# Seven products instead of eight for seven pairs of K tiles in the right half of a down projection

## The chip, the cores and the metric

The kernel runs on one core of a Trainium2 chip. The metric is the device time of one execution in microseconds; lower is better. TensorE is called PE here, VectorE DVE, ScalarE ACT, GpSimd POOL and SyncE SP, as in the profile.

## The reference

Two layers of a decoder trunk on 256 positions of width 2048, all in float32. The change touches the MLP at the end of each layer:

```python
hm = _rmsnorm(x, mlp_norm_g[l]) @ w_up[l]                # 256 x 2048 @ 2048 x 8192
x = x + jnp.square(jax.nn.relu(hm)) @ w_down[l]          # 256 x 8192 @ 8192 x 2048
```

Before it stand an attention and a short convolution with projections of their own (`w_in`, `w_out`); they are the same in both kernels.

## The kernel before

Every float32 matrix is split into a high part and a remainder, `hi` and `lo`, and a product is made of three matmuls (`TERMS`: hi by hi, hi by lo, lo by hi). ACT writes `hi` (a copy into a type that PE takes in one pass), DVE writes `lo = raw - hi`. The raw weights come by DMAs that SP issues.

The 256 rows are two tiles of 128, and K = 8192 is 64 tiles of 128, or 32 pairs of two. The MLP of a layer has these stages:

- The up loop, `for i in range(NP)` with NP = 32. A round makes one pair of activation tiles: two column blocks of `w_up` (`up_part`, L809), `evict` (L819, L820) and `square` (L826 to L841), which writes the squared tile to DRAM (`hid`, L831, on POOL's queue) and, for all but the last two pairs, four sums S1 to S4 of its quarters beside the quarters A11 to A22. It splits the eight into `f`.
- In the same loop, two rounds late (LAG = 2), the left half of the down projection (columns 0 to 1023 of `w_down`). A pair is a 2 by 2 block product: two row tiles, two K tiles, two column blocks of 512. Instead of eight products of 128x128 by 128x512 it takes seven (Strassen's scheme in Winograd's form), each of three matmuls (`product`, L849), into seven banks of PSUM. The weights' sums and differences are made by `quarters`: `plain` gives b11, b21 and b22 (tiles b1 and b2), `sums` gives t1 and t3 (t13), `more` gives t2 and t4 (t24). `t` is the tile of the raw sums. The raw pair is the tile `draw`, from a pool with two buffers (`dpool`).
- The last two pairs of the left half go by eight products (L935), straight onto the banks where four of the seven products add up. Then `onto` (L916) and, on POOL, four adds (L927) bring the seven banks into x.
- The right half (columns 1024 to 2047), by eight products for all 32 pairs (L969), in blocks of four K tiles (KG = 4). A block's activations are read back from `hid` (`block`: the tile `back`, split into `g`). A raw tile of 1 MB holds four K tiles by 512 columns, from `upool`, which has three buffers.

`Weights` is a queue of jobs; a job loads a raw tile where one begins and splits it. `take()` hands out the next job's tiles and makes jobs up to three further on (AHEAD). The tiles `whi` and `wlo` (a half of an ordinary pair) and `uhi` and `ulo` (`w_up`) share three buffers each, the tiles of `quarters` have one (b1 two), `f` two, `h` one.

PE's order is the order of the program. On the other engines and on SP a scheduler places each instruction by its estimate of when the operands and buffers are there; on the chip every engine then takes its instructions in that fixed order, and waits at the head of its queue.

Of the kernel before, what the change touches and what calls it, by code (L numbers as in the profile page):

```python
# [9 lines left out]
F32 = mybir.dt.float32  # L10
F32R = mybir.dt.float32r
# [4 lines left out]
P = 128  # L16
# [16 lines left out]
AHEAD = 3  # L33
NP = DFF // (2 * P)
LAG = 2
NB2 = DFF // (KG * P)

# [64 lines left out]
def trunk(ctx: ExitStack, tc: tile.TileContext, x, w_in, w_out, conv_w, q_norm_g, k_norm_g,  # L102
# [162 lines left out]
    class Weights:  # L265
# [3 lines left out]
        def __init__(self, pool):  # L269
            self.pool = pool  # L270
            self.jobs, self.made, self.used = [], [], 0
            self.early = []
# [394 lines left out]
    def mlp(l, mnorm, last):  # L667
# [3 lines left out]
        with ExitStack() as scope:  # L671
# [11 lines left out]
            def column(i, c, kh):  # L683
                def make():
                    if c == 0:
                        raws[kh] = upool.tile([P, 8, 2 * P], F32, tag="uraw", name="uraw")
                        nc.sync.dma_start(
                            raws[kh], w_up[l][kh * 8 * P:(kh + 1) * 8 * P,
                                              i * 2 * P:(i + 1) * 2 * P].rearrange(
                                                  "(k p) c -> p k c", p=P))  # L690
                    hi = wpool.tile([P, 8, P], F32R, tag="hi", name="uhi")
                    lo = wpool.tile([P, 8, P], F32R, tag="lo", name="ulo")
                    src = raws[kh][:, :, c * P:(c + 1) * P]
                    nc.scalar.activation(hi, src, AF.Copy)  # L694
                    nc.vector.tensor_sub(lo, src, hi.bitcast(F32))  # L695
                    return hi, lo
                weights.jobs.append(make)
# [8 lines left out]
            def quarters(i):  # L706


                keep = late if i == 0 else lambda ins: None
# [7 lines left out]

                def plain():
                    raw = forms["raw"] = load_rows(i, 0).rearrange("p k (n c) -> p k n c", n=2)
# [19 lines left out]
                if i == 0:  # L739
                    made = {}  # L740
                    begin = lambda: made.update(p=plain(), s=sums())
                    forms["begin"] = begin
                    return lambda: made["p"], lambda: made["s"], more
                return plain, sums, more

            def rows(i, k, box):
                def make():
                    if k == 0:
                        box.append(load_rows(i, 0))
                    return weights.halves(box[0][:, k].rearrange("p (n c) -> p n c", n=2))  # L750
                weights.jobs.append(make)
# [14 lines left out]
            for i in range(NP - LAG, NP):  # L766
                box = []
                rows(i, 0, box)
                rows(i, 1, box)

            order = [(b - n, n) for b in range(NB2 + 1) for n in range(2) if 0 <= b - n < NB2]

            def four(b, n, k, box):
                def make():
                    if k == 0:
                        raw = upool.tile([P, KG, CH], F32, tag="uraw", name="raw")
                        nc.sync.dma_start(
                            raw, w_down[l][b * KG * P:(b + 1) * KG * P,  # L780
                                           (2 + n) * CH:(3 + n) * CH].rearrange(
                                               "(k p) c -> p k c", p=P))
                        box.append(raw)
                    return weights.halves(box[0][:, k:k + 2])
                weights.jobs.append(make)

            for b, n in order:
                box = []
                four(b, n, 0, box)
                four(b, n, 2, box)  # L790


            hid = [dram.tile([P, KG * S], F32, name=f"hid{l}{b}") for b in range(NB2)]

# [27 lines left out]
            def square(i, h):  # L822
# [8 lines left out]
                nc.gpsimd.dma_start(hid[i // 2][:, i % 2 * 2 * S:(i % 2 + 1) * 2 * S], u)  # L831
                n = 4
                if i < NP - LAG:
                    n = 8
                    nc.vector.tensor_add(h[:, S1], h[:, A21], h[:, A22])
# [10 lines left out]
            def product(n, j, a, b, stop=False):  # L846

                for m, (pa, pw) in enumerate(TERMS):
                    nc.tensor.matmul(prods[n], fs[j][:, pa, a], b[pw], start=(j == 0 and m == 0),  # L849
                                     stop=(stop and m == 2))  # L850
# [49 lines left out]
            first.close()  # L900
            gpool = scope.enter_context(tc.tile_pool(name="gpool", bufs=3))
# [11 lines left out]
            blocks = {0: block(0)}  # L913

            def onto(dst, p, base):
                nc.vector.scalar_tensor_tensor(dst, p, mnorm.scale, base,  # L916
                                               op0=ALU.mult, op1=ALU.add)

            x11, x21, x12, x22 = (xs[n][:, t] for n in range(2) for t in range(NT))
            e1, e2, e3, e4 = wide("e1"), wide("e2"), wide("e3"), wide("e4")  # L920
            nc.scalar.activation(e1, prods[1], AF.Copy, scale=mnorm.scale)
            onto(e2, prods[6], e1)
            onto(e4, prods[5], e2)
            onto(x22, prods[5], x22)
            onto(e3, prods[7], e2)
            for dst, v in ((x11, e1), (x12, e4), (x21, e3), (x22, e3)):
                nc.gpsimd.tensor_tensor(dst, dst, v, op=ALU.add)  # L927

            prods[8] = ps.tile([P, CH], F32, tag="av", name=f"pr{l}8", bufs=1)
            for j in range(NP - LAG, NP):  # L930
                for k in range(2):
                    b = weights.take()
                    for n, t, p in ((0, 0, 2), (0, 1, 4), (1, 0, 3), (1, 1, 8)):
                        for m, (pa, pw) in enumerate(TERMS):
                            nc.tensor.matmul(  # L935
                                prods[p], fs[j][:, pa, 2 * k + t], b[pw][:, n],
                                start=(p == 8 and j == NP - LAG and k == 0 and m == 0),
                                stop=(j == NP - 1 and k == 1 and m == 2))
                    work.tick()
            for dst, p in ((x11, 2), (x21, 4), (x12, 3), (x22, 8)):  # L940
                onto(dst, prods[p], dst)

            def store(n):
                for t in range(NT):
                    nc.sync.dma_start(
                        out[0, t * P:(t + 1) * P, n * CH:(n + 1) * CH], xs[n][:, t])

            if last:
                store(0)
                store(1)  # L950
            else:
                work.start(norm.chunk(0, 2), 12)
                work.start(norm.chunk(1, 2), 24)


            accs = {}
            for b, n in order:
                if n == 0:
                    if b + 1 < NB2:
                        blocks[b + 1] = block(b + 1)  # L960
                if b == 0:
                    accs[n] = mm.tile([P, NT, CH], F32, tag="mm2", name=f"dn{l}{n}")
                f, acc = blocks[b], accs[n]
                for kp in range(KG // 2):
                    hi, lo = weights.take()
                    for k in (2 * kp, 2 * kp + 1):
                        for t in range(NT):
                            for m, (pa, pw) in enumerate(TERMS):
                                nc.tensor.matmul(  # L969
                                    acc[:, t], f[:, pa, k, t * P:(t + 1) * P],  # L970
                                    (hi, lo)[pw][:, k % 2],
                                    start=(b == 0 and k == 0 and m == 0),
                                    stop=(b == NB2 - 1 and k == KG - 1 and m == 2))
                        work.tick()
# [52 lines left out]
```

## Time and profile before

| | |
|---|---|
| median of 3 runs (lowest to highest) | 2178.97 us (2178.82 to 2180.45) |
| profiled execution | 2181.14 us, its span 2179.4 us |
| granted PE clock over the span | 0.999 |
| PE busy | 2156.6 us, 99% |
| DVE, ACT, POOL busy | 74%, 58%, 6% |
| moved by DMA | 446.62 MB, 205 GB/s |

The span is from the profiled execution's first instruction to its last; the rows of the profile count from its start. A busy PE is not PE at its peak, since matmuls overlap and their ends are modelled; so the pace of matmuls is read from their number in a stretch without a wait. The first layer's MLP lies at 400 to 1088 us (the right half of the down projection from 919), the second's from 1480 to the end.

### The profile page before, as it was taken

Reading aid. Unit: us, or ns where it says so; the run is one execution under the profiler, and the core shown is the slowest. Engines: PE = TensorE matmul, PEld = TensorE weight load, DVE = VectorE, ACT = ScalarE, POOL = GpSimd, SP = SyncE. Lnnn points to the kernel's source line nnn. Section 1 sums busy time; section 2 is a strip of 40 time slices with the busy share of each in tenths; the row PEclk is TensorE's granted clock in tenths of the full one; section 3 lists DMA queues with packets and bytes.
Section 4 is the critical chain, followed back from the end, with each engine's and each line's share of the span. In section 5 each row is a group of like instructions: output and inputs, shape, how many; then the busy total and the mean of one; then the engine's idle time right before and its main releaser. Section 6 shows DMA issues by size and latency. Waiting matters only on the chain.

```text
span 2179.4 us, 29050 instructions
## 1 busy us (share of the span) xinstructions
PE 2156.6 (99%) x11066; PEld 1828.6 (84%) x11066; DVE 1603.9 (74%) x2229; ACT 1271.7 (58%) x1718; POOL 138.8 (6%) x194
## 2 busy tenths in 40 slices
PE   8999999999999999999999999999999999999999
PEld 6888888888888888888888888888888888888887
DVE  6677655698888888855566776557988888887554
ACT  6456445566666666654454654455666666665443
POOL 2021100000000000100011111000000000001000
PEclk9999999999999999999999999999999999999999
DMA  7555656476666666587565466656766666666774
GB/s 256 180 156 177 218 185 184 157 238 223 213 212 215 220 208 214 189 277 241 175 205 181 156 199 197 184 173 190 225 218 217 213 212 216 219 208 212 246 242 145
DMA packets 292491, 446.62 MB, mean 205 GB/s; under 512 B 10403, under 2 KB 191221, under 8 KB 292352
## 3 DMA queue, kind: packets, MB, share of 16 engines
q1 hardware_dynamic: 285648, 423.66, 61.5%
q0 software_dynamic: 6656, 21.10, 2.6%
q8 instruction: 86, 1.41, 0.3%
q14 instruction: 53, 0.43, 0.1%
q10 hardware_dynamic: 48, 0.02, 0.0%
HBM read 425.84 MB, written 18.90 MB: 204 GB/s over the span
## 4 chain that ended last, share of the span: by engine, by line
PE 94%; DMA 2%; DVE 2%; ACT 1%; issue 1%; SPq 0%; DVEq 0%; ACTq 0%
PE upc L809 29%; PE dn L969 15%; PE pr L849 13%; PE o L338 8%; PE q L338 4%; PE gc L360 4%; PE ci L360 4%; PE k L338 4%; PE gb L360 4%; PE v L338 4%; PE upw L809 1%; DMA uraw<-in_w_up_dram 1%; PE sc L500 1%; PE av L536 1%; PE tpn L402 1%; DMA draw<-in_w_down_dram 1%
## 5 line engine op out<-in xcount | busy, mean ns | idle before, releaser
L283 DVE TENSOR_TENSOR wlo<-raw,whi 128x1024 fp32r<-128x1024 f32 (+1 forms) x386 | 473.3, 1228 | 385.5 <-ACT whi L282 381.0
L282 ACT ACTIVATE whi<-raw 128x1024 fp32r<-128x1024 f32 (+1 forms) x386 | 406.8, 1055 | 477.8 <-PE dn L969 166.7
L809 PE MATMUL upc<-nT,uhi 128*128 128x512 f32 x1920 | 477.5, 391 | 0.0
L694 ACT ACTIVATE uhi<-uraw 128x1024 fp32r<-128x1024 f32 x256 | 271.2, 1060 | 287.3 <-PE upc L809 253.9
L809 PEld LDWEIGHTS upc<-nT,uhi 128*128 128x128 f32 x1920 | 352.7, 188 | 68.2
L695 DVE TENSOR_TENSOR ulo<-uraw,uhi 128x1024 fp32r<-128x1024 f32 x256 | 312.8, 1222 | 115.3 <-ACT uhi L694 112.9
L969 PE MATMUL dn<-whi,g 128*128 128x512 f32 x1024 | 316.4, 389 | 0.0
L809 PEld LDWEIGHTS upc<-nT,ulo 128*128 128x128 f32 x1920 | 261.9, 190 | 18.7
L809 PE MATMUL upc<-nT,ulo 128*128 128x256 f32 x1920 | 267.7, 282 | 0.0
L969 PEld LDWEIGHTS dn<-whi,g 128*128 128x128 f32 x1024 | 192.2, 188 | 39.7
L969 PE MATMUL dn<-wlo,g 128*128 128x512 f32 x512 | 199.6, 390 | 1.1 <-DVE wlo L283 1.0
L338 PE MATMUL o<-whi,cat 128*128 128x512 f32 x512 | 159.6, 390 | 0.0
L969 PEld LDWEIGHTS dn<-wlo,g 128*128 128x128 f32 x512 | 96.1, 188 | 22.6 <-DVE wlo L283 2.8
L338 PEld LDWEIGHTS o<-whi,cat 128*128 128x128 f32 x512 | 96.2, 188 | 19.7
L338 PE MATMUL o<-wlo,cat 128*128 128x512 f32 x256 | 99.6, 389 | 0.0
L831 POOL DMA_DIRECT2D hid<-h x64 | 34.9, 545 | 949.1 <-ACT h L830 913.4
L849 PE MATMUL pr<-t13h,f 128*128 128x512 f32 x240 | 93.8, 391 | 0.0
L338 PE MATMUL q<-whi,nT 128*128 128x512 f32 x256 | 86.4, 406 | 4.1 <-ACT nT L248 4.1
L338 PE MATMUL k<-whi,nT 128*128 128x512 f32 x256 | 85.3, 399 | 0.0
L849 PE MATMUL pr<-t24h,f 128*128 128x512 f32 x240 | 84.0, 391 | 0.0
L849 PE MATMUL pr<-b2h,f 128*128 128x512 f32 x240 | 84.0, 391 | 0.0
L338 PE MATMUL v<-whi,nT 128*128 128x512 f32 x256 | 83.4, 396 | 0.0
(330 smaller groups left out, 3431.0 us busy)
## 6 DMA issues: line engine op xcount, KB each, us to landing
uraw<-in_w_up_dram SPq DMA_DIRECT2D x128, 1024.0 KB, 5.9
raw<-in_w_in_dram SPq DMA_DIRECT2D x192, 512.0 KB, 3.9
draw<-in_w_down_dram SPq DMA_DIRECT2D x64, 1024.0 KB, 5.1
raw<-in_w_down_dram SPq DMA_DIRECT2D x64, 1024.0 KB, 5.7
raw<-in_w_out_dram SPq DMA_DIRECT2D x64, 512.0 KB, 3.6
hid<-h POOLq DMA_DIRECT2D x64, 256.0 KB, 4.3
back<-hid SPq DMA_DIRECT2D x32, 512.0 KB, 3.3
rev<-by_dist_d POOLq DMA_DIRECT2D x4, 1024.0 KB, 11.1
```

Of the source, the lines that this page charges most:

```text
L282: nc.scalar.activation(hi[:, k], raw[:, k], AF.Copy)
L283: nc.vector.tensor_sub(lo[:, k], raw[:, k], hi[:, k].bitcast(F32))
L338: nc.tensor.matmul(acc[:, t], a.ap[:, pa, k % KG, t * P:(t + 1) * P], (hi, lo)[pw][:, j], start=(k == 0 and n == 0), stop=(k == nk - 1 and ...
L360: nc.tensor.matmul(acc[:, f, 0] if part else acc[:, f], wt[:, k % 4, fs], a.ap[:, 0, k % KG] if part else a.ap[:, :, k % KG], start=(part ...
L402: nc.tensor.transpose(tp[:, i * S + t * P:i * S + (t + 1) * P], xs[n][:, t, k * P:(k + 1) * P], ident)
L500: nc.tensor.matmul(sc[:, :W], qT[m * DK:(m + 1) * DK, a, i, t * P:(t + 1) * P], kT[m * DK:(m + 1) * DK, b, i, :W], start=(n == 0), stop=(n ...
L694: nc.scalar.activation(hi, src, AF.Copy)
L695: nc.vector.tensor_sub(lo, src, hi.bitcast(F32))
L809: nc.tensor.matmul(acc[:, 0] if part else acc, wt[:, k], a.ap[:, 0, k % KG] if part else a.ap[:, :, k % KG], start=(part == 0 and kh == 0 ...
L831: nc.gpsimd.dma_start(hid[i // 2][:, i % 2 * 2 * S:(i % 2 + 1) * 2 * S], u)
L849: nc.tensor.matmul(prods[n], fs[j][:, pa, a], b[pw], start=(j == 0 and m == 0), stop=(stop and m == 2))
L969: nc.tensor.matmul(acc[:, t], f[:, pa, k, t * P:(t + 1) * P], (hi, lo)[pw][:, k % 2], start=(b == 0 and k == 0 and m == 0), stop=(b == NB2 ...
```

## The change

- In the right half, the first 24 pairs (BLK = 12 blocks) are walked pair by pair, their raw tiles being `draw` tiles of 1 MB (two K tiles by 1024 columns). Pairs 2, 5, 8, 11, 14, 17 and 20 (SEVEN) go by the seven products, the other 17 by eight. Products 2, 3 and 4 add up in the same banks as the ordinary pairs; 1, 5, 6 and 7 have four banks of their own, which `seven_onto(2)` brings into x after pair 20. The last eight pairs go by blocks as before.
- The activations of a seven pair are read back as eight tiles (`hid7`, 512 KB, which `square` now writes for those pairs after S4), those of an ordinary pair as four (256 KB). Their splits go into `f`, two buffers; the read-back of a seven pair shares the buffer of `h`.
- The four adds of the left half's ending are on DVE instead of POOL, and so are those of the right half's.
- `take()` issues raw loads two jobs further ahead than it makes splits (MORE = 2); a job's load is a function of its own, `fetch`.
- The pools of the blocks (`gpool`) are opened after pair 20 instead of after the left half, and the next layer's norm of the left columns starts there.

```diff
+MORE = 2
+SEVEN = (2, 5, 8, 11, 14, 17, 20)
+BLK = 12
...
         def take(self):
             i = self.used
             self.used += 1
+            while self.fetched < min(len(self.jobs), i + 1 + AHEAD + MORE):
+                getattr(self.jobs[self.fetched], "fetch", lambda: None)()
+                self.fetched += 1
             while len(self.made) < min(len(self.jobs), i + 1 + AHEAD):
                 self.made.append(self.jobs[len(self.made)]())
             return self.made[i]
...
+            for i in range(2 * BLK):
+                if i in SEVEN:
+                    weights.jobs += quarters(i, 2 * CH)
+                else:
+                    rows(i, 2 * CH)
...
-                nc.gpsimd.dma_start(hid[i // 2][:, i % 2 * 2 * S:(i % 2 + 1) * 2 * S], u)
+                if i not in SEVEN:
+                    nc.gpsimd.dma_start(hid[i // 2][:, i % 2 * 2 * S:(i % 2 + 1) * 2 * S], u)
...
+                if i in SEVEN:
+                    nc.gpsimd.dma_start(hid7[i], h.rearrange("p a c -> p (a c)"))
...
+            def seven_onto(n):
+
+                x11, x21, x12, x22 = (xs[n + i][:, t] for i in range(2) for t in range(NT))
+                e1, e2, e3, e4 = wide("e1"), wide("e2"), wide("e3"), wide("e4")
+                nc.scalar.activation(e1, prods[1], AF.Copy, scale=mnorm.scale)
+                onto(e2, prods[6], e1)
+                onto(e4, prods[5], e2)
+                onto(x22, prods[5], x22)
+                onto(e3, prods[7], e2)
+                for dst, v in ((x11, e1), (x12, e4), (x21, e3), (x22, e3)):
+                    nc.vector.tensor_add(dst, dst, v)
+
+            def read_back(i):
+
+                n = 8 if i in SEVEN else 4
+                if i in SEVEN:
+                    back = fpool.tile([P, 8, P], F32, tag="h", name="back", bufs=1)
+                    nc.sync.dma_start(back.rearrange("p a c -> p (a c)"), hid7[i])
+                else:
+                    back = nat.tile([P, 4, P], F32, tag="wide", name="back")
+                    nc.sync.dma_start(back.rearrange("p a c -> p (a c)"),
+                                      hid[i // 2][:, i % 2 * 2 * S:(i % 2 + 1) * 2 * S])
+                f = fpool.tile([P, 2, 8, P], F32R, tag="f", name="f")
+                nc.scalar.activation(f[:, 0, :n], back, AF.Copy)
+                nc.vector.tensor_sub(f[:, 1, :n], back, f[:, 0, :n].bitcast(F32))
+                return f
...
+            for i in range(2 * BLK):
+                if i + 1 < 2 * BLK:
+                    fs[i + 1] = read_back(i + 1)
+                if i not in SEVEN:
+                    ordinary(i, (2, 4, 3, 8) if i == 0 else ())
+                    continue
+                if i == SEVEN[0]:
+                    for n in (1, 5, 6):
+                        prods[n] = bank(f"pr{l}r{n}")
+                    prods[7] = ps.tile([P, CH], F32, tag="av", name=f"pr{l}r7", bufs=1)
+                end = i == SEVEN[-1]
+                b11, b21, b22 = weights.take()
+                t1, t3 = weights.take()
+                t2, t4 = weights.take()
+                for n, a, b in ((1, A11, b11), (2, A12, b21), (3, S4, b22), (5, S1, t1),
+                                (7, S3, t3), (6, S2, t2), (4, A22, t4)):
+                    product(n, i, a, b, end and n in (1, 5, 6, 7),
+                            SEVEN[0] if n in (1, 5, 6, 7) else -1)
+                work.tick()
+                if end:
+                    seven_onto(2)
+                    if not last:
+                        work.start(norm.chunk(0, 2), 8)
+                        work.start(norm.chunk(1, 2), 16)
+                    first.close()
+                    gpool = scope.enter_context(tc.tile_pool(name="gpool", bufs=3))
+                    blocks = {BLK: block(BLK)}
```

More of the change, by code (lines that the diff above doesn't have):

```diff
@@ L737, in more, with begin, rows, fetch @@
                     return (h[:, 0], lw[:, 0]), (h[:, 1], lw[:, 1])
-                if i == 0:
+                if (i, col) == (0, 0):
                     made = {}
-                    begin = lambda: made.update(p=plain(), s=sums())
+                    def begin():
+                        fetch()
+                        made.update(p=plain(), s=sums())
                     forms["begin"] = begin
                     return lambda: made["p"], lambda: made["s"], more
+                plain.fetch = fetch
                 return plain, sums, more
-            def rows(i, k, box):
-                def make():
+            def rows(i, col):
+                def fetch():
+                    raws[i, "r"] = load_rows(i, col)
+                for k in range(2):
+                    def make(k=k):
+                        return weights.halves(
+                            raws[i, "r"][:, k].rearrange("p (n c) -> p n c", n=2))
                     if k == 0:
-                        box.append(load_rows(i, 0))
-                    return weights.halves(box[0][:, k].rearrange("p (n c) -> p n c", n=2))
-                weights.jobs.append(make)
+                        make.fetch = fetch
+                    weights.jobs.append(make)
             for i in range(NP):
@@ L766, in mlp, with four, fetch, make @@
             for i in range(NP - LAG, NP):
[L767 to L776, printed above, removed]
-                    if k == 0:
[L778 to L785, printed above, removed]
+                rows(i, 0)
+            for i in range(2 * BLK):
[3 more added lines that the diff above has]
+                    rows(i, 2 * CH)
+            order = [(b - n, n) for b in range(BLK, NB2 + 1) for n in range(2)
+                     if BLK <= b - n < NB2]
+            def four(b, n):
+                def fetch():
+                    raw = upool.tile([P, KG, CH], F32, tag="uraw", name="raw")
+                    nc.sync.dma_start(
+                        raw, w_down[l][b * KG * P:(b + 1) * KG * P,
+                                       (2 + n) * CH:(3 + n) * CH].rearrange(
+                                           "(k p) c -> p k c", p=P))
+                    raws[b, n, "b"] = raw
+                for k in (0, 2):
+                    def make(k=k):
+                        return weights.halves(raws[b, n, "b"][:, k:k + 2])
+                    if k == 0:
+                        make.fetch = fetch
+                    weights.jobs.append(make)
             for b, n in order:
-                box = []
-                four(b, n, 0, box)
-                four(b, n, 2, box)
+                four(b, n)
             hid = [dram.tile([P, KG * S], F32, name=f"hid{l}{b}") for b in range(NB2)]
+            hid7 = {i: dram.tile([P, 8 * P], F32, name=f"hid{l}s{i}") for i in SEVEN}
             def column_bank():
@@ L844, in mlp, with product, ordinary @@
             prods = {}
-            def product(n, j, a, b, stop=False):
+            def product(n, j, a, b, stop=False, start=0):
                 for m, (pa, pw) in enumerate(TERMS):
-                    nc.tensor.matmul(prods[n], fs[j][:, pa, a], b[pw], start=(j == 0 and m == 0),
-                                     stop=(stop and m == 2))
+                    nc.tensor.matmul(prods[n], fs[j][:, pa, a], b[pw],
+                                     start=(j == start and m == 0), stop=(stop and m == 2))
+            def ordinary(j, starts=(), stop=False):
+                for k in range(2):
+                    b = weights.take()
+                    for n, t, p in ((0, 0, 2), (0, 1, 4), (1, 0, 3), (1, 1, 8)):
+                        for m, (pa, pw) in enumerate(TERMS):
+                            nc.tensor.matmul(
+                                prods[p], fs[j][:, pa, 2 * k + t], b[pw][:, n],
+                                start=(p in starts and k == 0 and m == 0),
+                                stop=(stop and k == 1 and m == 2))
+                    work.tick()
             fs = {}
@@ new lines, in mlp, with store @@
+            seven_onto(0)
+            prods[8] = ps.tile([P, CH], F32, tag="av", name=f"pr{l}8", bufs=1)
+            for j in range(NP - LAG, NP):
+                ordinary(j, (8,) if j == NP - LAG else (), j == NP - 1)
+                if j == NP - LAG:
+                    fs[0] = read_back(0)
+            for n in range(2):
+                for t in range(NT):
+                    onto(xs[n][:, t], prods[((2, 4), (3, 8))[n][t]], xs[n][:, t])
+            def store(n):
+                for t in range(NT):
+                    nc.sync.dma_start(
+                        out[0, t * P:(t + 1) * P, n * CH:(n + 1) * CH], xs[n][:, t])
@@ L903, in block @@
+            if last:
+                store(0)
+                store(1)
             def block(b):
@@ L911, in block @@
                 return f
[L913 to L956, printed above, removed]
@@ L957, in mlp @@
-            for b, n in order:
[L958 to L962, printed above, removed]
+            accs = [mm.tile([P, NT, CH], F32, tag="mm2", name=f"dn{l}{n}") for n in range(2)]
+            prods[2], prods[4] = accs[0][:, 0], accs[0][:, 1]
+            prods[3], prods[8] = accs[1][:, 0], accs[1][:, 1]
+            for i in range(2 * BLK):
[16 more added lines that the diff above has]
+                            SEVEN[0] if n in (1, 5, 6, 7) else -1)
+                work.tick()
+                if end:
[6 more added lines that the diff above has]
+                    blocks = {BLK: block(BLK)}
@@ L963, in mlp @@
+            for b, n in order:
+                if n == 0 and b + 1 < NB2:
+                    blocks[b + 1] = block(b + 1)
                 f, acc = blocks[b], accs[n]
@@ L970, in mlp @@
                                     acc[:, t], f[:, pa, k, t * P:(t + 1) * P],
-                                    (hi, lo)[pw][:, k % 2],
-                                    start=(b == 0 and k == 0 and m == 0),
+                                    (hi, lo)[pw][:, k % 2], start=False,
                                     stop=(b == NB2 - 1 and k == KG - 1 and m == 2))
```

31 lines of the change are left out of this document (19 added, 12 removed).

## The prediction

> **What bounds the kernel now.** I read the page's head, its chain, TensorE's (PE's) waits, and a table by stage.
>
> ```profile
> span 2179.4 us, 29050 instructions
> PE 2156.6 (99%) x11066; PEld 1828.6 (84%) x11066; DVE 1603.9 (74%) x2229; ACT 1271.7 (58%) x1718; POOL 138.8 (6%) x194
> PE 94%; DMA 2%; DVE 2%; ACT 1%; issue 1%; SPq 0%; DVEq 0%; ACTq 0%
> ```
> ```profile
> 480.00:896.00 416.00, 414.98 (x2216) 358.48 (x2215) 369.65 (x499) 279.54 (x341) 14.60 (x27) 1.00 0.68 215
> 896.00:930.00 34.00, 32.54 (x151) 26.31 (x150) 24.58 (x25) 18.68 (x27) 5.65 (x5) 1.00 0.53 182
> 930.00:1088.00 158.00, 158.00 (x708) 131.02 (x707) 89.78 (x81) 77.10 (x82) 0.00 (x0) 1.00 0.68 230
> ```
> ```profile
> PE pr L849 <- DVE f L841: 3.2, 4, 1.0
> PE pr L935 <- DVE wlo L283: 1.6, 2, 0.8
> PE dn L969 <- DVE wlo L283: 1.0, 2, 0.6
> ```
> The columns of the second fence: stretch, its length, then PE, weight loads, DVE, ACT and POOL busy, granted clock, DMA share, GB/s. In the right half of the down projection (930 to 1088) PE never stops, DVE is busy 57% of it and DMA 68%. So time goes there only by matmuls, and time comes back only if something new stops PE. The pr and dn waits at the change from the up loop to the right half cost 1.3 us a layer, 2.6 in all.
>
> **What the matmuls give.** 128x512 matmuls show 390 ns each, but they overlap; their pace is in the chain in order of time:
> ```profile
> 957.33 130.58 PE dn L969 x576
> ```
> 130.58/576 = 0.2267 us. A seven pair takes 21 instead of 24: 3 x 7 pairs x 2 layers = 42 fewer, -9.5 us. An ordinary pair is 5.44 us, a seven pair 4.76, three pairs (two and one) 15.64.
>
> **What the extra work costs.** DVE's rows start closer together than they last:
> ```profile
> 624.71 0.42 DVE L828 TENSOR_TENSOR h<-h,ratiob 128x256 f32<-128x256 f32 x1
> 625.05 1.22 DVE L728 TENSOR_TENSOR t<-draw 128x1024 f32<-128x1024 f32 x1
> 626.18 1.22 DVE L695 TENSOR_TENSOR ulo<-uraw,uhi 128x1024 fp32r<-128x1024 f32 x1
> 627.32 0.69 DVE L731 TENSOR_TENSOR t<-t,draw 128x512 f32<-128x512 f32 x1
> 627.92 0.28 DVE L835 TENSOR_TENSOR h<-h 128x128 f32<-128x128 f32 x1
> ```
> ```profile
> 909.23 0.74 DVE L916 SCALAR_TENSOR_TENSOR x<-pr,rowf,x 128x512 f32<-128x512 f32 x1
> 909.89 0.73 DVE L916 SCALAR_TENSOR_TENSOR e<-pr,rowf,e 128x512 f32<-128x512 f32 x1
> ```
> A 1024-wide operation costs the queue 1.13 us (1.22 for one that is waited for), a 512-wide one 0.60 (0.69), one from PSUM 0.66. In three pairs DVE has nine 1024-wide (the two ordinary pairs' four halves; t, b2l, t13l, t24l and f of the seven pair) and five 512-wide operations (b1l, two of t, two f): 13.2 us of 15.64. DMA has three raw tiles and 1 MB read back: 4.2 MB in 15.64 us is 268 GB/s, by the window's 230 at 0.68 a share of 0.79. Neither is full. What matters is the order, for the raw tiles now have two buffers (dpool, draw) where the right half had three (upool).
> ```profile
> draw<-in_w_down_dram SPq DMA_DIRECT2D x64, 1024.0 KB, 5.1
> DMA to landing us min/median/max: 4.9/5.1/14.9
> DMA to landing us min/median/max: 5.4/5.9/13.4
> L282 ACT ACTIVATE whi<-raw 128x1024 fp32r<-128x1024 f32 x57 | 60.4, 1061 | 78.9 <-PE dn L969 73.1 <-DMA raw<-in_w_down_dram 5.7
> ```
> (Second row: draw; third: uraw, whose loads run two at a time.) From a buffer's release to data I take 5.1, draw's own median, + 0.1 to get issued = 5.2; the ends are 4.9 and uraw's 5.9. A landed ordinary tile is free again after ACT's first half 1.06 and DVE's two halves 1.13 + 1.22 = 3.41.
>
> I follow the order in which the built program's instructions stand and which load waits for which reader. Time 0 is the end of the up loop's products; p is an ordinary pair, S a seven pair, a and b a pair's halves. The left half's ending goes first on DVE; now it began here, against PE's first matmul after the products:
> ```profile
> 906.78 0.39 PE L935 MATMUL pr<-whi,f 128*128 128x512 f32 x1
> 907.02 0.75 DVE L916 SCALAR_TENSOR_TENSOR e<-pr,rowf,e 128x512 f32<-128x512 f32 x1 [0.41 <-ACT e L921]
> ```
> So from 0.24: four from PSUM, five 512-wide (four of them the adds that POOL did), one L828 at 0.34, then 31b 1.22: 7.4, under the 8.17 (36 matmuls) at which PE reaches 31b. The release of pair 31 starts p1's load at 7.5. From there one chain runs, each load waiting for the last reader before it:
> p1: load, 3.41. S2 (landed by then) and p3: t, b1l, t, b2l, t, f, t13l, 3a, t24l, 3b = 9.80. S5: load; t, 4b = 2.35. p6: load, 3.41. S8: load; t, b1l, t, b2l, t = 4.15. p9: load, 3.41. S11: load; t, b1l, b2l, t, f, t13l, t, 12a, 12b = 8.67. S14: load, 4.15. p15: load, 3.41. S17: load; t, b1l, t, 16b = 3.55. p18: load, 3.41. S20: load; t, 19b, t, b1l, b2l, t, t13l, f = 7.54.
> That is 7.5 + 11 loads x 5.2 + 57.3 = 122.0 until S20's activations are split. PE, never stopped, would start S20 after 16 ordinary and 6 seven pairs, 510 x 0.2267 = 115.6, and needs that f at the third matmul, 116.1. So PE comes 5.9 us late, a microsecond or two at a time, mostly on f and t24l. Queued behind each waiting load on SP are the next raw loads and read-backs; the read-backs of ordinary pairs stand one or more pairs ahead and are late for nobody.
>
> Behind S20 comes the seven products' ending. DVE still has t24l, 21a, 21b, f21, then the ending (four from PSUM, four adds, with 22a and 22b between), two splits of whole blocks (g) with 23a between, and only then f22: 8 x 1.13 + 5 x 0.60 + 4 x 0.66 + 0.69 = 15.4, until 137.4. PE, through S20 and p21 (from 121.5), wants f22 at 132.2: another 5.2 late. Were DVE not behind at all, it could begin when product 6 ends, 0.7 before the end of S20, and would need 9.65 from there; PE needs f22 5.9 after S20: 3.1 remain. So 11.1 us a layer, 22.2 in all; nothing later catches up, since PE is the bound there too.
>
> **Loading two jobs ahead.** In the up loop raw loads stand on SP in the same order as before, so this moves no load there. It does move DVE's order at the MLP's start. The third wait that PE had there:
> ```profile
> 478.94 1.22 DVE ulo L695
> 480.15 1.14 DVE t L728
> 481.29 1.15 DVE f L841
> 482.44 0.04 issue
> 482.48 2.57 PE pr L849 x10
> ```
> That f (pair 3's) now stands behind two more 512-wide operations and the next ulo: 0.60 + 1.13 + 0.60 = 2.3 later, in both layers; DVE has no gap there, so PE pays: +4.7. Between 0 (if DVE has caught up) and 4.7.
>
> **The rest at nothing.** Seven hid tiles become 512 KB on POOL's queue, issued after S4 instead of after Square, and h has one buffer, so DVE's next write of h may wait.
> ```profile
> hid<-h POOLq DMA_DIRECT2D x64, 256.0 KB, 4.3
> back<-hid SPq DMA_DIRECT2D x32, 512.0 KB, 3.3
> DVE ulo L695 <- ACT uhi L694: 45.6, 53, 1.4
> ```
> 512 KB takes 3.3 at the least, twice 4.3 at the most; I expect a wait near 1 us, hidden in DVE's 45.6 us of idle over 26 rounds (1.75 each; third row, window 480 to 896). Without that cover: up to 14 us. The left half's two ordinary pairs as the first users of both accumulators wait for their readers, 0.4 us, which the chain above covers.
>
> **Sum.** -9.5 + 22.2 - 2.6 + 4.7 = +14.8. The profiled execution took 2181.1 (span 2179.4), 2.2 above the median 2178.97; so 2195.9 against it, and 2194 for the median.
>
> By "DMA: Bandwidth & Descriptors" of the Trainium skill (Anatomy of one DMA), a load from POOL's queue costs about 2.0 us + bytes/436 GB/s, an estimate of 4.4 for 1 MB; draw's 64 loads here, from SP's, never took under 4.9, so the trace's figure stands in the sum. With 4.4 the chain would not bind, and it would be rival (2).
>
> **Rivals.**
> (1) Faster: the loads, alone on their queue without uraw beside them, come in time. The chain decides: it stops binding when a load takes 5.9/11 = 0.54 less, 4.6 or under. Then DVE is also not behind at S20, 3.1 a layer remain there, and if DVE has caught up at the start: -9.5 - 2.6 + 6.2 = -5.9, 2173. Against it: 4.9 is the shortest of 64.
> (2) No change: as (1), but the start's 4.7 is paid: -1.2, 2178.
> (3) Loads slower, since p15 and p16, p9 and p10, p18 and p19 and a 512 KB read-back are in flight together: 5.9 instead of 5.1 is 0.8 x 11 x 2 = +17.6, 2212. For it: DMA share 0.79 on average.
> (4) PE's clock falls in the gap at p22.
> ```profile
> 9.90 5.49 PE q L338 x12
> 16.54 5.49 PE q L338 x24
> ```
> After the long wait at the kernel's start the first 12 matmuls took 457 ns each, the next 24 229: 2.7 us lost. Twice that is +5.5, 2199. "TensorE: Matmul & The Clock Gate" of the Trainium skill (Why this matters for your kernels) warns of idle gaps over about 3 us between bursts, after which matmuls run at half rate; those rows agree, and the waits of 1.0 us and less elsewhere cannot show it.
>
> **How the numbers follow.** About 0.2% (4.4 us) is what a measurement can tell from no change. Forecast 0.47, own range 2186 to 2203 (load of 4.9: -4.4; start free: -4.7; up); (1) 0.12; (2) 0.11; (3) 0.14; (4) 0.16. Low 2175 leaves out most of (1); high 2213 takes in (3). Faster 0.12; same 0.13 (case 2 and an edge of the forecast); slower 0.75.
>
> **What would show it.** Right: in the changed profile PE has 42 fewer matmuls; new PE waits on DVE f and t24l of about 6 us a layer among the seven pairs; one wait of about 5 us a layer at p22, the second pair after the last seven pair; ACT's b1h or DVE's t waiting on draw's landing, S tile to S tile 17 to 18 us against 15.64 in the rounds from S14 on. Wrong: PE idle under 4 us a layer there, or draw landing at 4.5 or less; or the loss lying in the up loop (h waiting on hid).

## The result and the profile after

The changed kernel takes 2218.7 us (median of 2214.5, 2217.2, 2220.3 and 2227.1) against 2179.3 for the kernel before: 1.0184 times, 95% interval 1.0168 to 1.0199. The forecast was 2194, its range 2175 to 2213. The sign was right and the size was not: +39.5 us instead of +14.8. The profiled execution of the changed kernel is its fastest one (2214.5, span 2212.7), so its trace shows +33.4 against the profiled execution of before; the other executions took 3 to 13 us more, and no trace here holds these.

The head of the page and the chain:

```profile
span 2212.7 us, 29198 instructions
PE 2162.5 (98%) x11024; PEld 1823.1 (82%) x11024; DVE 1679.5 (76%) x2347; ACT 1310.9 (59%) x1772; POOL 129.5 (6%) x186
PE 84%; DMA 8%; DVE 6%; ACT 1%; issue 1%; POOL 0%; SPq 0%; DVEq 0%; ACTq 0%
draw<-in_w_down_dram SPq DMA_DIRECT2D x112, 1024.0 KB, 5.5
```

PE has 42 matmuls fewer (11066 before) and yet more busy time: the work is less, but part of it runs slower. DMA has 8% of the chain instead of 2%. The stages, in the columns of the prediction's table (stretch, its length, PE, weight loads, DVE, ACT, POOL busy, granted clock, DMA share, GB/s):

```profile
480.00:896.00 416.00, 414.95 (x2213) 358.61 (x2213) 369.15 (x495) 285.22 (x340) 14.58 (x27) 1.00 0.70 218
896.00:930.00 34.00, 33.32 (x152) 27.02 (x151) 25.79 (x33) 15.08 (x19) 0.54 (x1) 1.00 0.74 248
930.00:1088.00 158.00, 143.77 (x613) 113.98 (x612) 115.09 (x123) 86.66 (x107) 0.00 (x0) 0.98 0.64 219
```

In the right half PE was busy 158.00 of 158 us; now it is 143.77, at a granted clock of 0.98. DVE's share went up to 73% and DMA's went down from 0.68 to 0.64: neither is full, they wait for each other. The chain through that stretch in layer 0 (start, us, what) is one of loads that wait for a buffer, and ends at seven pair 20's activations (shown in part):

```profile
910.56 1.20 DVE x L962 x2
911.76 1.15 DVE wlo L289
912.92 7.27 DMA draw<-in_w_down_dram
...
923.76 5.89 DMA draw<-in_w_down_dram
...
934.34 5.48 DMA draw<-in_w_down_dram
...
1023.16 5.30 DMA draw<-in_w_down_dram
...
1034.99 1.15 DVE f L976
1036.14 0.04 issue
1036.18 0.50 PE pr0r L884
```

The chain holds 11 loads, 63.25 us in all (63.35 in layer 1). PE in the order of time, at pair 22 (start, us, operation, and in brackets the idle time before it and what ended it):

```profile
1036.18 0.50 PE L884 MATMUL pr0r<-b1h,f 128*128 128x512 f32 x1 [1.20 <-DVE f L976]
...
1045.88 0.39 PE L894 MATMUL dn<-whi,f 128*128 128x512 f32 x1
1050.51 0.80 PE L894 MATMUL dn<-whi,f 128*128 128x512 f32 x1 [4.25 <-ACT f L975]
1051.11 0.63 PE L894 MATMUL dn<-wlo,f 128*128 128x512 f32 x1
1052.23 1.22 PE L894 MATMUL dn<-whi,f 128*128 128x512 f32 x2 [0.49 <-DVE f L976]
1053.25 0.63 PE L894 MATMUL dn<-wlo,f 128*128 128x512 f32 x1
1053.67 1.06 PE L894 MATMUL dn<-whi,f 128*128 128x512 f32 x2
```

The forecast wait is there, and behind it the matmuls last 0.63 us and start 0.43 apart, where 0.39 and 0.2267 are usual. The granted clock (stretch, length, PE busy, clock, DMA share, GB/s) says why, in layer 0 and in layer 1:

```profile
1050.40:1054.00 3.60, 2.99 (x6) 0.50 0.77 262
1054.00:1058.00 4.00, 4.00 (x13) 0.68 0.04 16
1058.00:1062.00 4.00, 4.00 (x19) 1.00 0.00 0
...
2150.00:2154.00 4.00, 2.96 (x6) 0.50 0.72 217
```

One more loss lies in the up loops' start, at pair 3:

```profile
479.38 0.50 PE L884 MATMUL pr<-b1h,f 128*128 128x512 f32 x1 [1.63 <-ACT f L875]
...
481.16 0.50 PE L884 MATMUL pr<-b1h,f 128*128 128x512 f32 x1 [1.05 <-DVE f L876]
```

A loss is counted below as the distance between the starts of two matmuls less 0.2267, since the idle time in brackets leaves out the overlap that a wait breaks (1.20 idle is 1.36 lost).

### The profile page after: what moved, and what is told of

Read it like the earlier page. It is cut to its first block, busy times and chain, and to the rows that moved or that the text cites. A ratio compares the mean times of both kernels' runs of the same rounds, so it can differ in the third digit from the quotient of the medians.

```text
span 2212.7 us, 29198 instructions
## 1 busy us (share of the span) xinstructions
PE 2162.5 (98%) x11024; PEld 1823.1 (82%) x11024; DVE 1679.5 (76%) x2347; ACT 1310.9 (59%) x1772; POOL 129.5 (6%) x186
## 4 chain that ended last, share of the span: by engine, by line
PE 84%; DMA 8%; DVE 6%; ACT 1%; issue 1%; POOL 0%; SPq 0%; DVEq 0%; ACTq 0%
PE upc L841 29%; PE pr L884 13%; PE o L347 8%; DMA draw<-in_w_down_dram 6%; PE q L347 4%; PE gc L369 4%; PE ci L369 4%; PE gb L369 4%; PE v L347 4%; PE dn L1049 4%; PE k L347 4%; DVE wlo L289 2%; PE dn L894 1%; PE upw L841 1%; DMA uraw<-in_w_up_dram 1%
## 5 line engine op out<-in xcount | busy, mean ns | idle before, releaser
L289 DVE TENSOR_TENSOR wlo<-raw,whi 128x1024 fp32r<-128x1024 f32 (+1 forms) x290 | 356.0, 1229 | 281.1 <-ACT whi L288 276.7
L288 ACT ACTIVATE whi<-raw 128x1024 fp32r<-128x1024 f32 (+1 forms) x290 | 305.3, 1053 | 354.1 <-PE o L347 73.6
L894 PE MATMUL dn<-whi,f 128*128 128x512 f32 x544 | 176.1, 399 | 12.2 <-ACT f L975 8.2
L894 PEld LDWEIGHTS dn<-whi,f 128*128 128x128 f32 x544 | 103.6, 192 | 39.2 <-ACT f L975 9.7
L289 DVE TENSOR_TENSOR wlo<-draw,whi 128x1024 fp32r<-128x1024 f32 x76 | 91.5, 1221 | 51.4 <-ACT whi L288 51.4
L894 PE MATMUL dn<-wlo,f 128*128 128x512 f32 x272 | 108.6, 399 | 3.0 <-DVE wlo L289 3.0
L744 DVE TENSOR_TENSOR t<-draw 128x1024 f32<-128x1024 f32 x74 | 90.2, 1219 | 22.1 <-DMA draw<-in_w_down_dram 22.1
L728 DVE TENSOR_TENSOR t24l<-t,t24h 128x1024 fp32r<-128x1024 f32 x74 | 90.5, 1222 | 2.9
L728 DVE TENSOR_TENSOR t13l<-t,t13h 128x1024 fp32r<-128x1024 f32 x74 | 90.4, 1222 | 2.4 <-ACT t13h L727 0.5
L728 DVE TENSOR_TENSOR b2l<-draw,b2h 128x1024 fp32r<-128x1024 f32 x74 | 90.0, 1216 | 0.1
```

The costliest lines, as they stand in the source:

```text
L288: nc.scalar.activation(hi[:, k], raw[:, k], AF.Copy)
L289: nc.vector.tensor_sub(lo[:, k], raw[:, k], hi[:, k].bitcast(F32))
L728: keep(nc.vector.tensor_sub(lo, src, hi.bitcast(F32)))
L744: keep(nc.vector.tensor_sub(t[:, 0:2], raw[:, :, 1], raw[:, 0]))
L894: nc.tensor.matmul(prods[p], fs[j][:, pa, 2 * k + t], b[pw][:, n], start=(p in starts and k == 0 and m == 0), stop=(stop and k == 1 and m ...
```

## The experiments

Theory A: the raw tiles with their two buffers stop PE. Theory C: at pair 22 it is the place of f22 behind the ending. Against them stood the order of conversions on DVE, and the clock as a cause of its own. Each ratio is against the kernel before on the same chip (medians of 2179.4 to 2179.8, so chips differ by half a microsecond at most); differences to the changed kernel are differences of medians.

**Five raw buffers (e1).**

```diff
 def rows(i, col):
     def fetch():
-        raws[i, "r"] = load_rows(i, col)
+        raws[i, "r"] = (upool tile "uraw", named praw) if col else load_rows(i, col)
```

> The ordinary pairs of the right half take their raw tiles from upool's three buffers, the seven pairs keep dpool's two: five raw buffers instead of two, everything else as changed. Theory A (raw tiles): the 12 us a layer that PE loses before the last seven pair come from loads that wait for a raw buffer, so they go, and with them the slow matmuls at that pair in layer 1 (1.8 us); DVE is also less behind at pair 22. 2218.7 - 24 - 2 - 2 to 6 = 2187 to 2191. Rival B (order of conversions): PE waits on f and t24l because these stand behind other conversions in DVE's queue, whatever the buffers: at least 8 us a layer stay, 2210 or more.

2200.8 us, ratio 1.0087 (1.0070 to 1.0103): 18 us less than the changed kernel, not 28 to 32. The stretch 940 to 1050 (same columns as above), first of this kernel:

```profile
940.00:1050.00 110.00, 109.89 (x485) 90.65 (x483) 91.97 (x94) 68.83 (x82) 0.00 (x0) 1.00 0.66 227
```

and of the changed one:

```profile
940.00:1050.00 110.00, 97.56 (x416) 76.72 (x414) 88.21 (x94) 62.85 (x78) 0.00 (x0) 1.00 0.65 221
```

PE never stops, with the same products, conversions and read-backs, and DVE does more in the same time: A holds and B falls. (The build also gives DVE another order here; that the buffers held the changed kernel up is seen in its chain, which is one of loads.) The wait at 22 is only 0.55 us for ACT and 0.80 for DVE (0.78 and 0.80 in layer 1), without slow matmuls: most of it was DVE's lag from the raw tiles. What came instead is PE's wait at the change of halves:

```profile
920.40 0.84 PE L901 MATMUL pr<-whi,f 128*128 128x512 f32 x2 [3.66 <-DVE f L883]
934.40 0.80 PE L901 MATMUL dn<-whi,f 128*128 128x512 f32 x1 [5.76 <-DVE x L956]
```

```profile
923.74 0.69 DVE L748 TENSOR_TENSOR t<-draw,t 128x512 f32<-128x512 f32 x1
927.92 0.69 DVE L728 TENSOR_TENSOR b1l<-draw,b1h 128x512 fp32r<-128x512 f32 x1 [3.50 <-ACT b1h L727]
...
930.01 0.75 DVE L956 SCALAR_TENSOR_TENSOR x<-pr,rowf,x 128x512 f32<-128x512 f32 x1
```

(PE first, then DVE.) Seven pair 2's raw tile has a buffer earlier, and the order of DVE's queue, fixed when the program is built, then puts its conversions, and one of pair 5's, ahead of the left half's ending, which frees the banks of the first right pair. DVE idles 3.5 us at its head for a tile that has not landed.

**f22 ahead of the ending (e2).**

```diff
-    if end: seven_onto(2); ...; first.close(); gpool = ...; blocks = {BLK: block(BLK)}
+    if i == SEVEN[-1] + 1: seven_onto(2); ...          # behind read_back(i + 1)
+    if i == SEVEN[-1] + 2: first.close(); gpool = ...; blocks = {BLK: block(BLK)}
```

> The seven products' ending in the right half is issued one pair later, behind the split of pair 22, and the first whole block is read back and split one pair after that; nothing else. Theory C (tail): PE's wait at pair 22 (4.9 and 4.7 us) is the place of f22 behind the ending and the g splits on DVE and ACT, and the slow matmuls after it (2.9 and 2.5 us, 400 ns instead of 227) are a consequence of that gap: both go, 2218.7 - 15 = 2204. Rival D: the wait at 22 is only DVE's lag from the raw tiles, and moves to pair 23 or to the first block: 2214 or more. Rival E: the clock falls for another reason (the sum of the short waits before): the wait goes and the slow matmuls stay, 2209.

2205.7 us, 1.0115 (1.0098 to 1.0132): 13.0 less than the changed kernel, C's 15 within its noise. PE has no wait at pair 22 (one of 0.75 us a pair later in layer 1), and the clock stays at 1.00:

```profile
1050.00:1058.00 8.00, 8.00 (x36) 6.27 (x35) 8.00 (x10) 6.44 (x7) 0.00 (x0) 1.00 0.51 193
```

So the slow matmuls there followed from the gap. D and E fall. The trace gave something else, in layer 1's raw-tile part:

```profile
2044.58 0.51 PE L884 MATMUL pr1r<-t24h,f 128*128 128x512 f32 x1 [1.08 <-ACT t24h L727]
2046.30 0.69 PE L884 MATMUL pr1r<-t24l,f 128*128 128x512 f32 x1 [1.22 <-DVE t24l L728]
2046.78 0.63 PE L884 MATMUL pr1r<-t24h,f 128*128 128x512 f32 x1
```

Two waits of little more than 1 us, 1.7 us apart, were enough for 3.5 us of slow matmuls; the two waits of the changed kernel's start in layer 0 (1.63 and 1.05, shown above) were not. The clock's experiment below shows why.

**No look-ahead (e3):** `MORE = 0`.

> MORE = 0: raw tiles are loaded as far ahead as before the change, with seven pairs as changed. Theory F (start): the 3.4 us that PE lost at the start of the two up loops come from the order that the look-ahead gives DVE, and in the right half the two buffers, not the look-ahead, hold the loads: 2218.7 - 3.4 = 2215. Rival G: the look-ahead hides loads in the right half, without it each of 11 chained loads is later by the issue behind a conversion (about 1 us): 2218.7 - 3.4 + 20 = 2235.

2217.5 us, 1.0171 (1.0156 to 1.0186): 1.2 less than the changed kernel, inside both intervals. G falls, since the right half did not get slower. F falls too, for its own reason: the start's waits are still there. These are this kernel's lines; the changed kernel had 1.63 and 1.05:

```profile
481.84 0.50 PE L884 MATMUL pr<-b1h,f 128*128 128x512 f32 x1 [1.63 <-ACT f L875]
...
484.01 0.50 PE L884 MATMUL pr<-b1h,f 128*128 128x512 f32 x1 [1.44 <-DVE f L876]
```

**No seven pair in the right half (e4):** `SEVEN = ()`, the ending left out, block 12 set up behind pair 20.

> The right half's first 24 pairs go pair by pair from dpool's two buffers as changed, but all of them by eight products: no seven pairs, no ending in the right half, no 512 KB tiles written and read. It leaves 42 matmuls in. Theory A: an ordinary pair holds a buffer for 5.75 + 3.4 = 9.2 us, so two buffers give a pair each 4.6 us, under the 5.44 that PE takes: no wait, 2179.3 + 3.4 (start) - 3.7 (the old waits at the change of halves) = 2179. Rival H (two buffers are too few for any walk by pairs, or the read-backs of 256 KB come late): more than 2190.

2182.7 us, 1.0009 (1.0000 to 1.0019). PE is busy 158.00 of 158 us from 930 to 1088: two buffers are enough for a walk by ordinary pairs, and H falls. The start's new waits are gone with the seven pairs (0.66 and 0.99 us on f, as in the kernel before). The old waits at the change of halves (3.7 us) do not simply go: in their place stands one wait of 1.9 us a layer for the left half's ending, with some 1.7 us of slow matmuls after it in layer 1.

**Only the 512 KB tiles, in the kernel before (e7).**

```diff
-    nc.gpsimd.dma_start(hid[...], u)                     # every pair, behind Square
+    if i not in SEVEN: nc.gpsimd.dma_start(hid[...], u)
     ... S1 to S4 ...
+    if i in SEVEN: nc.gpsimd.dma_start(hid7[i], h)       # 512 KB
```

> The kernel before, with only the hidden tiles changed: the seven pairs' tiles are written as 512 KB behind S4, the right half reads the first half of each back (256 KB each). Theory I: the start's loss of the changed kernel comes here too, f of pair 3 late in both layers: 2179.3 + 3.4 + 1.3 = 2184. Rival F (the split of fetch and conversion makes it): 2179.3.

2186.5 us, 1.0032 (1.0020 to 1.0044): +7.1, more than the 4.7 of theory I, and nothing of the rival. The waits of the changed kernel are there, in a kernel that has no look-ahead and no seven pair in the right half:

```profile
481.72 0.50 PE L854 MATMUL pr<-b1h,f 128*128 128x512 f32 x1 [1.72 <-ACT f L845]
...
484.05 0.50 PE L854 MATMUL pr<-b1h,f 128*128 128x512 f32 x1 [1.59 <-DVE f L846]
```

The way to it is on DVE. In the kernel before pair 3's two evictions stand right behind an ulo:

```profile
466.23 1.22 DVE L695 TENSOR_TENSOR ulo<-uraw,uhi 128x1024 fp32r<-128x1024 f32 x1
467.37 0.76 DVE L820 TENSOR_TENSOR h<-ev 128x256 f32<-128x256 f32 x2
```

With the longer and later write out of the one `h` buffer (8.2 us from issue to landing in the changed kernel between 440 and 500, 4.8 for 256 KB before) they stand behind five more operations, an order that is fixed when the program is built (e7's lines):

```profile
464.59 1.22 DVE L696 TENSOR_TENSOR ulo<-uraw,uhi 128x1024 fp32r<-128x1024 f32 x1
465.72 1.22 DVE L729 TENSOR_TENSOR t<-draw 128x1024 f32<-128x1024 f32 x1
...
470.59 0.69 DVE L716 TENSOR_TENSOR b1l<-draw,b1h 128x512 fp32r<-128x512 f32 x1 [0.77 <-ACT b1h L715]
471.20 0.76 DVE L822 TENSOR_TENSOR h<-ev 128x256 f32<-128x256 f32 x2
```

**The clock by itself (e8).** In the kernel before, at chosen places of the right half:

```diff
+    copy(read, read)            # VectorE; waits until PE has read that weight tile
+    max(s1, ...) x (m + 1)      # m = 0 to 8
+    next_f = s1 * 0 + next_f    # what PE needs next
```

> The kernel before, with waits put into PE's work in the right half: a chain of VectorE operations on a scratch tile that starts when PE has read a weight tile and ends in the next tile it needs. Layer 0: single gaps of about 1, 2, 2, 3, 4, 4, 5 and 6 us, 16 us apart. Layer 1: four gaps of about 1 us, 2.7 us of work apart; four of about 2; three of about 2 to 3 us, 5.4 us of work apart; one of 3 and one of 4. Theory J (only a long gap): matmuls start 427 ns apart instead of 227 after every gap of 3.5 us or more and after none below. Theory K (share of a stretch of time): also after gaps of 1 to 2 us where several stand close together, and after some single gaps of 2 to 3 us and not others, as in the changed kernel's seven pair 20 of layer 1 (1.9 us).

2281.3 us, one execution. Idle time of PE before the matmul, and whether matmuls after it started 0.43 us apart:

| idle us | slow matmuls behind it |
|---|---|
| 0.75, five times, four of them 3.7 apart | none |
| 1.48, three times | none |
| 2.17, 2.34, 2.57 | after each, 1.5 to 1.7 us lost |
| 3.2 to 7.6, eleven times | after each, 1.4 to 2.8 us lost |

The gap of 2.17 us ended at 966.5, and the rate fell only about 1 us later (same columns as above):

```profile
964.19:967.60 3.41, 1.24 (x6) 0.96 (x6) 3.02 (x6) 1.06 (x1) 0.00 (x0) 1.00 0.61 196
967.60:971.01 3.41, 3.41 (x10) 2.63 (x9) 0.26 (x1) 0.00 (x0) 0.00 (x0) 0.50 0.65 187
```

J falls: gaps far under 3.5 us do it. Of K, the single gaps of 2 to 3 us bear it out; its four short gaps in a row did not slow PE, at 0.75 us each. In the other kernels gaps of 1.8 to 2.1 us did it in some places and not in others: 1.92 and 1.90 us in the two layers of e4, not in the first, but in the second.

The granted clock tells these apart. In every trace its slow stretches begin on one grid of 3.413 us, which keeps its phase through the whole execution, and each lasts one or two steps of it. These are three steps of e4, one in layer 0 and two in layer 1:

```profile
920.60:924.01 3.41, 1.70 (x7) 1.42 (x8) 3.41 (x6) 1.82 (x2) 0.00 (x0) 1.00 1.03 411
1999.22:2002.63 3.41, 1.51 (x6) 0.93 (x6) 3.41 (x5) 0.76 (x1) 0.00 (x0) 1.00 1.03 417
2002.63:2006.04 3.41, 3.41 (x9) 2.65 (x9) 3.24 (x5) 2.42 (x3) 0.00 (x0) 0.50 1.04 405
```

The wait of 1.92 us falls on two steps, 1.71 of it in the one shown, and the clock stays; the wait of 1.90 lies in one step whole, and the next step is slow. So it goes in all 13 profiled executions (their first 30 and last 8 us left out). With losses counted as above and added up within a step, the full-clock step ahead of each of the 40 slow stretches lost 2.01 us or more; of the 8106 other full-clock steps none lost more than 1.97. In e8 the four gaps of 0.75 us lie 3.7 us apart, so no step held two of them. "TensorE: Matmul & The Clock Gate" of the Trainium skill (Why this matters for your kernels) sets the bound at gaps over about 3 us, and (Part 1) describes free-running windows of some 3.4 us. The first is too high for these traces; the second agrees with their steps of 3.413 us.

**Buffers and tail together (e5).** e2, and e1 for pairs from 3 on only (`if col and i > SEVEN[0]`).

> Both at once: ordinary pairs from pair 3 on take their raw tiles from upool's three buffers (pairs 0 and 1 stay on dpool, so that seven pair 2 is converted no earlier than in the changed kernel), and the right half's ending stands behind f22. Theories A and C: the raw-tile waits (12 us a layer) and the tail (7 us a layer) go, and the waits that five buffers brought at the change of halves do not come. From before: 2179.3 - 9.5 - 3.7 + 0.9 (first wait on the left half's ending stays) + 3.4 and 1.3 (start of the up loop) = 2172; from the changed kernel by the parts measured singly: 2218.7 - 25 - 13 = 2181. So 2172 to 2181. Rival L (the waits at the change of halves come with any earlier load): 2190 or more.

2179.5 us, 0.9998 (0.9989 to 1.0007): 39 us less than the changed kernel and no different from before. Together they give more than singly (18 + 13), for the waits at the change of halves do not come back: L falls.

**Then where the first seven pair stands (e6, e9 to e11).** e6 leaves out seven pair 2.

> The same without seven pair 2 (SEVEN = 5, 8, 11, 14, 17, 20): six matmuls more. Theory I: what PE lost at the start of the up loops (3.4 us and 1.3 of slow matmuls) is the 512 KB write of pair 2 out of the single h buffer, which puts the next pair's evictions behind five conversions on DVE; from pair 5 on DVE has room. 3.3 us below e5. Rival M (any seven pair costs that, wherever it stands): the start's loss moves to pair 6, and the time is 1.4 above e5.

2184.1 us, 1.0022 (1.0012 to 1.0031): 4.6 above e5, though the start is clean (0.67 and 0.99 us on f). Neither I nor M: PE waits elsewhere, at seven pair 5.

```profile
949.70 0.50 PE L891 MATMUL pr0r<-t24h,f 128*128 128x512 f32 x1 [1.15 <-ACT t24h L727]
953.47 0.79 PE L891 MATMUL pr0r<-t24l,f 128*128 128x512 f32 x1 [3.27 <-DVE t24l L728]
```

t24l stood behind b1l and b2l of pair 8 in DVE's queue, and PE ran slow there in both layers. e9 gives ordinary pairs upool's buffers from pair 3 on, not from 6, which moves seven pair 5 earlier:

> As e6 (six seven pairs, the first is pair 5), but ordinary pairs take upool's buffers from pair 3 on instead of pair 6 on, so that seven pair 5 gets dpool's buffer two pairs earlier. In e6 PE waited 1.2 and 3.3 us (0.7 and 3.2 in layer 1) for the last products of seven pair 5, whose t24l stood on DVE behind the first conversion of pair 8's raw tile, and ran slow after it; in this kernel's order t24l stands ahead of that conversion. If that is the cause: e6's 2184 less 4.9 + 4.3 of waits and 2 to 3 us of slow matmuls twice = 2170. If DVE is simply full there: 2180 or more.

2173.6 us, 0.9971 (0.9961 to 0.9980): faster than both kernels (0.3% under the one before), with six seven pairs, 3.6 above what I expected. Eight seven pairs, from 5 and from 4:

> As e9 with eight seven pairs: 5, 8, ... 26, and the pair walk over 30 pairs (BLK = 15), one block left. 12 matmuls fewer than e9, 2.7 us: 2167 if e9 gives 2170; it beats the kernel before by 0.5%. If the ending beside the last block and layer 1's norm has no room, PE waits again near pair 28 and the gain goes: 2172 or more.

> As e10 with seven pairs 4, 7, ... 25: the first one nearer to the change of halves, the ending one pair earlier. Same products as e10: the same time, 2167, if neither end binds; more where pair 4's conversion comes ahead of the left half's ending on DVE (as in e1) or the 512 KB write of pair 4 still meets a full DVE at the start of the up loop (up to +5).

2174.5 (0.9975, 0.9966 to 0.9984) and 2175.4 (0.9981, 0.9973 to 0.9990): no better than e9, in spite of 12 matmuls fewer. In e10 PE waits 2.5 us in the next layer's norm and is slow behind it (2.97 us in e11), so the gain goes at another place than the expected pair 28:

```profile
1100.98 0.96 PE L411 MATMUL tpn<-ident,x 128*128 128x128 f32 x4 [2.50 <-DVE nT L254]
```

## Why the prediction was wrong, step by step

**The mechanisms were mostly right, two of the sizes were not, and two rivals that were priced as alternatives came together.** In the order of the steps, from the profiled executions:

- Products, -9.5: right. 42 matmuls fewer, at 0.2267 us.
- Raw-tile chain, 5.9 a layer: mis-sized. PE's third matmul of seven pair 20 began 130.7 us after the end of the up loop's products in layer 0 (1036.18 - 905.45) and 129.9 in layer 1, against the 116.1 it would take unstalled: 14.6 and 13.8. The start was right (7.47 against 7.5). The step that failed is "from a buffer's release to data I take 5.1 + 0.1": the 11 loads took 63.25 us, 5.75 each, not 57.2 in all. The seven that had another raw load in flight beside them for 4 us or more took 5.9 to 7.8 (the first: DMA share 0.94 from 913 to 921), the others 5.0 to 5.9, but for one of 6.6. From seven pair to seven pair DVE's first t stood 18.8 and 17.7 us apart at the end of layer 0 (forecast 17 to 18). The median of another stage was carried into one where the loads meet others; rival (3) named this and had 5.9, +0.8 a load where it was +0.55. Another 2.6 us in layer 0 and 1.8 in layer 1 are gaps between the chain's conversions, which the sum took as closed.
- Tail, 5.2 a layer: right in place and size (4.9 and 4.6), as the sum of two causes. e1 shows that without the raw-tile lag 1.7 to 1.9 remain (forecast 3.1, with a need of 9.65 whose steps the forecast does not list), e2 that the order alone can hide it. The steps followed DVE alone, but in both layers the wait ended on ACT's half of f22 (4.25 and 3.99 us), and DVE's half cost PE 0.49 more. Ahead of f22 on ACT stood eight of the next norm's operations in layer 0, and in layer 1 2.09 us of waiting for a block's read-back.
- The clock, rival (4): +5.5 for the two gaps at pair 22, measured 2.9 + 2.5. Right, but it was put beside the forecast as another case, while it is a consequence of the gap that the forecast itself contained. The forecast also had no slow matmuls elsewhere: layer 1 lost 1.8 more at seven pair 20 (a wait of 1.93 us) and 1.4 at the start.
- Old transition waits, -2.6: -3.7 when counted between starts.
- Start, +4.7: 1.1 and 2.2 and the 1.4 of slow matmuls, so the sum was right and the reason wrong. "Loading two jobs ahead" is not what makes these waits (e3); the 512 KB write behind S4 is (e7). The failed step is "a wait near 1 us, hidden in DVE's 45.6 us of idle": that idle time was read from 480 to 896, and the write of the first seven pair meets DVE ahead of it, where the changed kernel has DVE busy 20.00 of 20 us (460 to 480).
- Program start: 2.4 us earlier in the profiled execution, where the change does nothing.

-9.5 + 28.4 + 9.5 + 8.6 - 3.7 + 3.3 - 2.4 = +34.2; the trace has +33.4. Of the 19.4 over the forecast's sum 16.6 are the raw tiles and 8.6 the clock; the other terms are 5.8 under it. Rivals (1) and (2) fell: no load in the chain took under 4.99.

What stays open: how much of the longer loads is due to which neighbour (no run took one away alone); whether the size of the 512 KB write or its later place costs the start its time (e7 has both); and what POOL's four adds on DVE cost, which was not tried by itself.

## What to carry to other kernels

Rivals that can be true at the same time are terms, not cases: the slower load made the gap, and the gap made the slow clock, and the range has to hold their sum. Before a new user shares a buffer, ask for the time that each user holds it, in this stage's traffic: two raw buffers were enough for ordinary pairs (e4) and 12 us a layer short for a mix with seven pairs. In a queue whose order is fixed when the program is built, an earlier load can cost as much as a late one, since its conversions move ahead of what PE needs first (e1, e6); so a buffer is added together with a look at what overtakes what.

## What the hardware showed

The granted clock was halved by what PE lost within one step of a fixed grid of 3.413 us, not by the length of a single gap: in these traces 2.01 us or more lost in a step made the next one slow, and 1.97 or less did not. So two waits of 1.1 and 1.2 us in one step did it (e2), while a gap of 1.97 us that fell on two steps did not (e2, layer 1), and the clock fell up to 1.1 us after a gap had ended (e8: 966.5 and 967.60). A second slow step followed where PE idled 0.64 us or more in the first (15 times), none where it idled 0.58 or less (40 times). In all it cost 1.4 to 2.9 us beyond the wait itself. The grid's phase against the program differed between the executions, so a wait near 2 us on PE can cost almost twice its length in one and only itself in another: at the start of its first MLP the kernel before lost 2.0 us at one matmul without a slow step, and e1 lost 1.9 at the same place with one.
